# Scalings by roots a slot later, gate product and first taps on VectorE, short copies on ScalarE, and taps queued behind a slot's jobs

## The chip, the cores and the metric

The kernel runs on one core of a Trainium2 chip. The metric is device time in microseconds. Engines: TensorE (PE for its matmuls, PEld for its weight loads), VectorE (DVE), ScalarE (ACT), GpSimd (POOL) and SyncE (SP), which issues the DMAs here. Each engine runs its instructions in the order in which the program queued them and waits on semaphores for the results of other engines.

## The reference, cut to what matters

One layer of a streaming encoder for 256 prompt frames and 64 frames of a running stream, 2048 channels wide, in float32:

```python
h = rmsnorm(x, g_pre_mix)
p = h @ w_in
# group A: Conformer convolution on 1024 channels
u = p_val * sigmoid(p_gate)
u = causal_dwconv(u, state, w_dw, width 31) + b_dw
a = silu(layernorm per token and per group of 128 channels(u) * gn_g + gn_b)
# group B: gated DeltaNet, 8 heads of 128
qkv = silu(causal_dwconv(p_qkv, state, w_sc, width 4))
q, k = l2norm(q), l2norm(k)
o, s = gated delta rule in chunks (q, k, v, decay, beta, state)
b = rmsnorm per head(o) * onorm_g * silu(z)
x = x + rmsnorm(concat(a, b) @ w_out, g_post_mix)
h = rmsnorm(x, g_pre_ffn)
gate, up = split(causal_dwconv(h @ w_up, state, width 3) + b_ffn_dw)
x = x + rmsnorm((silu(gate) * up) @ w_down, g_post_ffn)
```

The outputs are x and the new states: the last 30 rows of u, the last 3 rows of q/k/v before their convolution, the delta rule's state, and the last 2 up-projected rows.

## The kernel before

Channels lie on the 128 partitions and the T = 320 frames (256 + 64) along the free axis. Each weight block of 128 x 1024 is loaded by DMA and split on the chip into a high part (`whi`, a ScalarE copy, L196) and a low part (`wlo`, a VectorE subtraction, L197); three matmuls a tile (L212, L213, L216) make a product near float32. These are the dense matmuls. A block of `w_in` has 48 of them, one of `w_out` in the mixer's stage 33.

**Jobs between the dense matmuls.** The mixer's small matmuls and transposes are not a stage of their own. They are generators ("jobs": `conv_tail`, `gdn_tail`, `pair` with `levels` and `post`) that advance between dense matmuls. `tick` counts the dense matmuls. At every 20th (`GAP`), a slot, it advances each job that is due, at most one step each, its TensorE instructions queued behind the last dense matmul and its priority raised. A `yield wait, g, t` says in how many dense matmuls the next step is due, and how many PSUM banks of the pools `ps_g` (4) and `ps_t` (2) that step takes; a step that finds too few waits for the next slot, and banks of `ps_t` count for the following slot too. The instructions of one engine are ordered at compile time by priority and estimated readiness; on the chip each engine then keeps to that order.

**Convolutions.** `conv_block(b)` computes gate and value of 128 channels. The normalisation's row factor `rb` multiplies both. The sigmoid is 0.5 tanh(x/2) + 0.5: VectorE scales the gate (L512), ScalarE takes tanh (L513), GpSimd makes the sigmoid and multiplies by `rb` (L514, L515), and VectorE multiplies by the value in PSUM (L521) into the buffer `ub`, whose 5 segments of 94 columns each begin with the 30 columns before it. GpSimd copies the saved rows (L520) and the overlaps (L523). The 31 taps (`cvt` and `odd`, two accumulators) and their sum are the list `taps`: the first on ScalarE (L536), the rest on VectorE (L538, L539, L533). `tick` hands out `pace` taps a slot: 3, 1 during the heads' projections, 4 at the end. `finish_conv(b - 3)` hands out what remains before the buffer is used again. `conv_tail(b)` waits until all taps are handed out, then 40 dense matmuls, transposes the sum (L554), takes mean and variance on VectorE, the root on GpSimd (L562, L563) and scales on ScalarE to `un` (L566); 100 dense matmuls later it transposes back (L570).

**Heads.** `qkv_block` evicts a q, k or v block to `qb`, copies its last rows to `nqkv` (L603, L604, GpSimd) and the saved rows into `qb` (L600, GpSimd) and applies 4 taps. `gdn_tail` transposes q, k, v, takes sums of squares on ScalarE, the inverse root and five products on GpSimd (L663 to L669), scales `kd`, `vh`, `kds` on ScalarE (L672 to L677), and 30 dense matmuls later multiplies keys by queries (`pk`, `pks`, L681, L685). When both heads of a pair are there, `pair` inverts a triangular matrix (`base_inverse`, `levels`: L755 to L800) and `post` runs the delta rule's two chunks (L827 to L884), takes a root on GpSimd (L893 to L897), scales `ot` on ScalarE (L899), and 120 dense matmuls later transposes the outputs (L909).

The blocks follow `PLAN`: z is a gate block, g the decays, h a head, c a convolution.

```python
PLAN = "z0 z1 g h0 h1 c0 h2 z2 h3 c1 z3 c2 h4 h5 c3 h6 h7 c4 z4 c5 z5 z6 c6 z7 c7"
```

After them come 15 blocks of `w_out` over the mixer outputs that are ready, then the rest of `w_out`, and the feed-forward part, which the change does not touch. From h4 on, a pair's first head forces the pair two before it on until it is `free`.

Of the kernel before, what the change touches and what calls it, by code (L numbers as in the profile page):

```python
# [9 lines left out]
F32 = mybir.dt.float32  # L10
F32R = mybir.dt.float32r
AF = mybir.ActivationFunctionType
ALU = mybir.AluOpType
# [4 lines left out]
P = 128  # L18
# [4 lines left out]
T = TP + TS  # L23
# [7 lines left out]
GAP = 20  # L31
# [8 lines left out]
LAG_NORM = 120  # L40
LAG_WAIT = 12
# [59 lines left out]
def trunk_kernel(ctx, tc, ins, outs):  # L101
    nc = tc.nc
    V, S, G, PE = nc.vector, nc.scalar, nc.gpsimd, nc.tensor
# [7 lines left out]
    dense = [None, 0]  # L111
# [3 lines left out]

    taps, pace = [], [3]

    def next_tap():
        left, fn = taps.pop(0)
        with tc.issue_after(dense[0]):  # L120
            fn()
        left[0] -= 1

# [18 lines left out]
    def tick(mm):  # L142
        dense[0] = mm.ins
        dense[1] += 1
        if dense[1] % GAP == 0:
            g, t0, behind = 0, held_t[0], dense[0]
            t = t0
            for job in sorted(jobs, key=lambda j: j[0]):
                if job[0] <= dense[1] and g + job[2] <= 4 and t + job[3] <= 2:
                    g += job[2]  # L150
                    t += job[3]
                    behind = advance(job, behind)
            held_t[0] = t - t0
            for _ in range(min(pace[0], len(taps))):
                next_tap()

    const = ctx.enter_context(tc.tile_pool(name="const", bufs=1))
    wst = ctx.enter_context(tc.tile_pool(name="wst", bufs=3))
# [12 lines left out]
    def pv(name, a=None, b=None):  # L171
        o, w = PAR[name]
        if a is None:
            return par[:, o:o + w]
        return par[:, o + a:o + (a + 1 if b is None else b)]
# [84 lines left out]
    rb = act.tile([P, T], F32, tag="rb", name="rb")  # L260
# [31 lines left out]
    with tc.tile_pool(name="xp", bufs=1) as xp:  # L292
# [25 lines left out]
        with tc.high_priority(offset=PRI_E):  # L318
# [25 lines left out]
            for k in range(KB):  # L344
                x = xt[k // 4][:, k % 4, :]
# [18 lines left out]
        for k0 in range(0, KB, 2):  # L364
            hi, lo = pre[k0 // 2]
            for ks in ((k0,), (k0 + 1,)) if k0 < 4 else ((k0, k0 + 1),):
                for wt in (hi, lo):
                    for k in ks:
                        for i, b in enumerate(FIRST):
                            ps = ready[b][:, 0:T]  # L370
                            o = (k - k0) * FW + i * P
                            w = wt[:, o:o + P]
# [15 lines left out]
    cb = pa.enter_context(tc.tile_pool(name="cb", bufs=2, reuse_waits="tile"))  # L388
# [103 lines left out]
    nqkv = const.tile([P, 24, 2, 3], F32, tag="nqkv", name="nqkv")  # L492

    ubufs = [cb.tile([P, 5, 94], F32, tag=f"ub{i}", bufs=1, name=f"ub{i}") for i in range(3)]
    for u in ubufs:
# [2 lines left out]
    def finish_conv(b):  # L500
        while any(left is lefts[b] for left, _ in taps):
            next_tap()
        finish(convs[b])
# [3 lines left out]
    def conv_block(b):  # L507
        psg_ = in_block(8 + b, "psgate")
        ub = ubufs[b % 3]
        with tc.high_priority(offset=PRI_E):  # L510
            sg = cb.tile([P, T], F32, tag="sg", bufs=1, name="sg")
            V.tensor_tensor(sg, psg_[:, 0:T], rb, ALU.mult)  # L512
            S.activation(sg, sg, AF.Tanh, scale=0.5)  # L513
            G.tensor_scalar(sg, sg, 0.5, 0.5, ALU.mult, ALU.add)  # L514
            G.tensor_tensor(sg, sg, rb, ALU.mult)  # L515
        psv = in_block(b, "psv")
        if b > 2:
            finish_conv(b - 3)
        with tc.high_priority(offset=PRI_E):
            G.tensor_copy(ub[:, 4, 0:30], pv("s_conv", b * 30, (b + 1) * 30))  # L520
            V.tensor_tensor(ub[:, :, 30:94], psv[:, 0:T].rearrange("p (s i) -> p s i", s=5),  # L521
                            sg.rearrange("p (s i) -> p s i", s=5), ALU.mult)
            G.tensor_copy(ub[:, 1:4, 0:30], ub[:, 0:3, 64:94])  # L523
        for i in range(2):
            nc.sync.dma_start(outs["conv"][:, b, i, :], ub[:, 3 + i, 64:94])

        cvt = cb.tile([P, 5, 64], F32, tag="cvt", bufs=3, name="cvt")
        odd = cb.tile([P, 5, 64], F32, tag="odd", bufs=1, name="odd")
        left = [32]

        def tap(t):
            if t == 31:
                return lambda: V.tensor_tensor(cvt, cvt, odd, ALU.add)  # L533
            x, acc, w = ub[:, :, t:t + 64], (cvt, odd)[t % 2], pv("w_dw", b * 31 + t)
            if t == 0:
                return lambda: S.activation(acc, x, AF.Identity, scale=w, bias=pv("b_dw", b))  # L536
            if t == 1:
                return lambda: V.tensor_scalar(acc, x, w, None, ALU.mult)  # L538
            return lambda: V.scalar_tensor_tensor(acc, x, w, acc, ALU.mult, ALU.add)  # L539

        lefts[b] = left
        taps.extend((left, tap(t)) for t in range(32))
        return cvt.rearrange("p s i -> p (s i)"), left

    def conv_tail(b, cvt, left):
        while left[0]:
            yield GAP, 0, 0
        yield LAG_CONV, 0, 1
        pt = ps_t.tile([P, 512], F32, tag="t", name="pt_c")
        st = cb.tile([P, 3, 6], F32, tag="bst", name="bst")  # L550
        gv = cb.tile([P, 3, 2], F32, tag="gvar", name="gvar")

        for c, o in enumerate((0, 128, 192)):
            PE.transpose(pt[:, c * P:(c + 1) * P], cvt[:, o:o + P], cv("ident"))  # L554
        for c in range(3):
            V.bn_stats(st[:, c, :], pt[:, c * P:(c + 1) * P])
            V.bn_aggr(gv[:, c, :], st[:, c, :])
        rs = cb.tile([P, 3], F32, tag="grs", name="grs")
        nm = cb.tile([P, 3], F32, tag="gnm", name="gnm")
        V.tensor_scalar(rs, gv[:, :, 1], EPS, None, ALU.add)  # L560
        V.tensor_scalar(nm, gv[:, :, 0], -1.0, None, ALU.mult)
        G.tensor_tensor(rs, rs, nhalf[:, 0:3], ALU.pow)  # L562
        G.tensor_tensor(nm, nm, rs, ALU.mult)  # L563
        un = cb.tile([P, 3, P], F32, tag="un", bufs=1, name="un")
        for c in range(3):
            S.activation(un[:, c, :], pt[:, c * P:(c + 1) * P], AF.Identity, scale=rs[:, c:c + 1], bias=nm[:, c:c + 1])  # L566
        yield LAG_STAT, 0, 1
        pt2 = ps_t.tile([P, 512], F32, tag="t", name="pt_c2")
        for c, o in ((2, 192), (1, 128), (0, 0)):
            PE.transpose(pt2[:, o:o + P], un[:, c, :], cv("ident"))  # L570
        af = cb.tile([P, T], F32, tag="t320", bufs=2, name="af")
        S.activation(af, pt2[:, 0:T], AF.Silu, scale=pv("gn_g", b), bias=pv("gn_b", b))
        split_mix(b, af)
# [22 lines left out]
    def qkv_block(b, dst, dsts, i):  # L596
        psq = in_block(16 + b, "psq")
        qb = qbufs[i % 2]
        with tc.high_priority(offset=PRI_E):
            G.tensor_copy(qb[:, 259:262], pv("s_qkv", b * 3, b * 3 + 3))  # L600
            V.tensor_tensor(qb[:, 3:259], psq[:, 0:TP], rb[:, 0:TP], ALU.mult)
            V.tensor_tensor(qb[:, 262:326], psq[:, TP:T], rb[:, TP:T], ALU.mult)
            G.tensor_copy(nqkv[:, b, 0, :], qb[:, 256:259])  # L603
            G.tensor_copy(nqkv[:, b, 1, :], qb[:, 323:326])  # L604
            cq = cb.tile([P, 323], F32, tag="cq", name="cq")
            S.activation(cq, qb[:, 0:323], AF.Identity, scale=pv("w_sc", b * 4))
            for t in range(1, 4):
                V.scalar_tensor_tensor(cq, qb[:, t:t + 323], pv("w_sc", b * 4 + t), cq, ALU.mult, ALU.add)
            S.activation(dst, cq[:, 0:TP], AF.Silu)
            S.activation(dsts, cq[:, TP + 3:TP + 3 + TS], AF.Silu)  # L610

# [14 lines left out]
    def gdn_tail(h, st, kq, vT):  # L626
        s = h % NS
# [39 lines left out]
        G.tensor_tensor(snb, rk, gate["nbeta"][:, 0:nch, h], ALU.mult)  # L667
        G.tensor_tensor(snb, snb, rk, ALU.mult)
        G.tensor_tensor(cc, rk, gate["beta"][:, 0:nch, h], ALU.mult)  # L669
        for c in range(nch):  # L670
            if c < 2:
                S.activation(kd[:, i0 + c, :], tk[c], AF.Identity, scale=skd[:, c:c + 1])  # L672
            else:
                for e in range(2):
                    r = slice(e * TS, (e + 1) * TS)
                    S.activation(kds[r, e, :], tk[c][r, :], AF.Identity, scale=skd[r, c:c + 1])
            S.activation(vh[:, i0 + c, :], tvs[c], AF.Identity, scale=irk[:, c:c + 1])  # L677
# [124 lines left out]
    def post(i, st):  # L802
# [39 lines left out]
        p = bank("ks", 4)  # L842
# [8 lines left out]
        p = outputs(0, vn0)  # L851
# [3 lines left out]
        p = bank("pvns", 1)  # L855
# [6 lines left out]
        p = bank("ks1", 4)  # L862
# [8 lines left out]
        p = bank("pos", 3)  # L871
# [11 lines left out]
        p = outputs(1, vn1)  # L883
# [11 lines left out]
        G.tensor_scalar(t1, t1, 1.0 / P, EPS, ALU.mult, ALU.add)  # L895
        G.tensor_tensor(t1, t1, nhalf[:, 0:NI], ALU.pow)
        G.tensor_tensor(t1, t1, rq, ALU.mult)  # L897
        for a in range(NI):
            S.activation(ot[:, a, :], ot[:, a, :], AF.Identity, scale=t1[:, a:a + 1])  # L899
        st["free"] = True  # L900
        yield LAG_NORM, 0, 2
        while any(zT[h] is None for h in hh_):
            yield GAP, 0, 2
        for s in range(2):
# [31 lines left out]
    for step in plan:  # L936
        kind, i = step[0], int(step[1:] or 0)
# [6 lines left out]
        elif kind == "h":  # L944
            if i % NS == 0:
# [4 lines left out]
                st = {}  # L950
# [32 lines left out]
    acc = None  # L983
# [144 lines left out]
    for q in range(NQ):  # L1128
# [5 lines left out]
        for j in range(QB):  # L1134
            b = q * QB + j
# [152 lines left out]
```

## Time and profile before

| | |
|---|---|
| median of 3 runs | 1509.2 us (1506.81 to 1511.67) |
| the profiled execution | 1509.19 us, span 1507.4 us |
| granted TensorE clock, mean | 0.995 |
| busy share of the span | PE 99%, PEld 97%, DVE 66%, ACT 48%, POOL 20% |
| HBM | 215.33 MB read, 7.12 MB written, 148 GB/s |

The profile lists, for each engine, what was busy when, how long it sat idle before an instruction and which other engine's instruction ended that idle time. A row of instructions in order of time gives its start and length in us, the engine, the line, the operation, the tiles (out<-in), the shapes and the count, and in brackets the idle time before it. A row of a group gives count, then busy us and mean ns of one, then the idle us before them. A row of waits gives who waited for whom: us in total, times, longest. The mixer's stage, in which all the changed lines run, lies between about 60 and 510 us.

### The profile page before, as it was taken

To read this page: it belongs to the slowest core of one execution; us is meant where nothing else is said; L and a number is where in the kernel's file an instruction comes from. 1 tells how busy PE (TensorE), PEld (TensorE's weight loads), DVE (VectorE), ACT (ScalarE), POOL (GpSimd) and SP (SyncE) were. 2 spreads that over 40 slices of the span, in tenths; PEclk is the share of its full clock that TensorE was granted. 3 is DMA by queue.
4 is the path that set the end of the run, shared out by engine and by line. 5 is a ranking of instruction groups with operands and counts; after the bars stand their busy time and mean duration, and the time that the engine had idled before them with its cause. 6 is when DMAs were issued, how large, how long until landed. Compare 5 with 4: busy or idle time off the path is not lost.

```text
span 1507.4 us, 27312 instructions
## 1 busy us (share of the span) xinstructions
PE 1486.2 (99%) x10609; PEld 1463.3 (97%) x10610; DVE 997.8 (66%) x1856; ACT 716.2 (48%) x1217; POOL 306.3 (20%) x492
## 2 busy tenths in 40 slices
PE   9999999999999999999999999999999999999998
PEld 8999998989899989999999999999999999999997
DVE  6798797879996568865435666545665545666554
ACT  7664555554454565544434444334444333444453
POOL 0333332441110000322002222001322101322101
PEclk9999999999999999999999999999999999999999
DMA  8335353455335654444454444455444455444453
GB/s 291 137 128 176 117 158 102 118 161 144 119 89 160 194 166 151 143 150 133 143 163 157 151 152 141 138 147 173 147 154 150 125 151 176 142 153 154 128 153 117
DMA packets 98281, 224.22 MB, mean 149 GB/s; under 512 B 18792, under 2 KB 39528, under 8 KB 98152
## 3 DMA queue, kind: packets, MB, share of 16 engines
q1 hardware_dynamic: 98008, 222.45, 46.4%
q8 instruction: 83, 1.36, 0.4%
q14 instruction: 46, 0.38, 0.1%
q10 hardware_dynamic: 144, 0.03, 0.0%
HBM read 215.33 MB, written 7.12 MB: 148 GB/s over the span
## 4 chain that ended last, share of the span: by engine, by line
PE 80%; DVE 11%; ACT 3%; issue 2%; DMA 2%; POOL 2%; SPq 0%; ACTq 0%; DVEq 0%
PE psu L216 13%; PE psu L213 13%; PE psu L212 13%; PE psdn L212 6%; PE psdn L213 6%; PE psdn L216 6%; DVE wlo L197 3%; PE psm L213 2%; PE psm L216 2%; PE psm L212 2%; PE psq L216 2%; PE psq L212 2%; PE psq L213 2%; PE psu L1081 1%; DVE odd L539 1%
## 5 line engine op out<-in xcount | busy, mean ns | idle before, releaser
L196 ACT CAST whi<-w 128x1024 fp32r<-128x1024 f32 (+2 forms) x440 | 412.9, 940 | 500.7 <-PE psu L213 168.5
L197 DVE TENSOR_TENSOR wlo<-w,whi 128x1024 fp32r<-128x1024 f32 (+2 forms) x440 | 478.0, 1087 | 200.8 <-ACT whi L196 125.8
L213 PE MATMUL psu<-lo,whi 128*128 128x320 f32 x1344 | 397.0, 309 | 0.0
L212 PE MATMUL psu<-hi,whi 128*128 128x320 f32 x1344 | 397.0, 309 | 0.0
L213 PEld LDWEIGHTS psu<-lo,whi 128*128 128x128 f32 x1344 | 252.3, 188 | 0.0
L212 PEld LDWEIGHTS psu<-hi,whi 128*128 128x128 f32 x1344 | 252.3, 188 | 0.0
L216 PE MATMUL psu<-hi,wlo 128*128 128x320 f32 x1344 | 224.4, 309 | 0.0
L1114 POOL COPY nffn<-fbuf 128x2 f32<-128x2 f32 x88 | 100.4, 1141 | 586.9 <-DVE fbuf L1112 583.7
L216 PEld LDWEIGHTS psu<-hi,wlo 128*128 128x128 f32 x1344 | 204.0, 188 | 0.0
L213 PE MATMUL psdn<-gl,whi 128*128 128x320 f32 x660 | 195.9, 310 | 0.0
L1112 DVE TENSOR_TENSOR fbuf<-psu,rb 128x256 f32<-128x256 f32 x88 | 37.4, 425 | 169.3 <-PE psu L216 169.3
L212 PE MATMUL psdn<-gh,whi 128*128 128x320 f32 x480 | 142.8, 309 | 0.0
L213 PEld LDWEIGHTS psdn<-gl,whi 128*128 128x128 f32 x660 | 123.9, 188 | 0.3
L212 PE MATMUL psq<-hh,whi 128*128 128x320 f32 x352 | 106.3, 315 | 0.0
L213 PE MATMUL psq<-hl,whi 128*128 128x320 f32 x352 | 104.1, 309 | 0.0
L212 PEld LDWEIGHTS psdn<-gh,whi 128*128 128x128 f32 x480 | 90.1, 188 | 0.0
L216 PE MATMUL psdn<-gh,wlo 128*128 128x320 f32 x480 | 89.9, 309 | 0.0
L216 PEld LDWEIGHTS psdn<-gh,wlo 128*128 128x128 f32 x480 | 75.3, 188 | 0.0
L212 PEld LDWEIGHTS psq<-hh,whi 128*128 128x128 f32 x352 | 66.1, 188 | 0.3
L213 PEld LDWEIGHTS psq<-hl,whi 128*128 128x128 f32 x352 | 66.1, 188 | 0.2
L539 DVE SCALAR_TENSOR_TENSOR cvt<-ub,par,cvt 128x320 f32<-128x320 f32 x120 | 66.1, 551 | 0.1
L539 DVE SCALAR_TENSOR_TENSOR odd<-ub,par,odd 128x320 f32<-128x320 f32 x112 | 62.1, 555 | 0.0
(360 smaller groups left out, 2516.7 us busy)
## 6 DMA issues: line engine op xcount, KB each, us to landing
w<-in_w_up SPq DMA_DIRECT2D x176, 512.0 KB, 3.7
w<-in_w_in SPq DMA_DIRECT2D x88, 512.0 KB, 3.7
w<-in_w_down SPq DMA_DIRECT2D x64, 384.0 KB, 3.1
w<-in_w_down SPq DMA_DIRECT2D x64, 320.0 KB, 2.9
w<-in_w_out SPq DMA_DIRECT2D x32, 320.0 KB, 2.9
w<-in_w_out SPq DMA_DIRECT2D x16, 384.0 KB
w<-in_w_first SPq DMA_DIRECT2D x6, 512.0 KB, 5.6
wtp<-wsp SPq DMA_DIRECT2D x4, 640.0 KB
```

Source lines behind the costliest of these rows:

```text
L196: S.copy(hi[:, 0:width], w[:, 0:width])
L197: V.tensor_tensor(lo[:, 0:width], w[:, 0:width], hi[:, 0:width].bitcast(F32), ALU.subtract)
L212: tick(PE.matmul(ps, wh, xh, start=(first and k0 + j == 0), stop=False))
L213: tick(PE.matmul(ps, wh, xl, start=False, stop=False))
L216: tick(PE.matmul(ps, lo[:, j * P:(j + 1) * P], xh, start=False, stop=(final and k0 + j == nk - 1)))
L539: return lambda: V.scalar_tensor_tensor(acc, x, w, acc, ALU.mult, ALU.add)
L1081: PE.matmul(pss[i][:, 0:T], wt[:, o:o + P], x, start=(k == 0 and n == 0), stop=(k == KB - 1 and n == 2))
L1112: V.tensor_tensor(buf[:, 2:258], psu[:, 0:TP], rb2[:, 0:TP], ALU.mult)
L1114: G.tensor_copy(nffn[:, b, 0, :], buf[:, 256:258])
```

## The change

- `next_tap` takes an instruction `front`, and queues the tap behind it. `tick` looks up the last VectorE instruction that the slot's jobs issued; the slot's taps go behind that one. Before, the edge named the last dense matmul.
- The product with the gate: (tanh + 1) x (value x 0.5 `rb`), two VectorE operations, with `rbh` = 0.5 `rb` made once on ScalarE. The two GpSimd operations go.
- The first tap goes from ScalarE to VectorE.
- The copies into `ub` and `qb`, and those to `nqkv` (two merged into one, after the taps), go from GpSimd to ScalarE.
- `conv_tail`, `gdn_tail` and `post` yield once more, for 12 dense matmuls (one slot), between the root on GpSimd and the scalings on ScalarE; in `post`, `free` is set before that and the lag after it is a slot shorter.

```diff
@@ -115,9 +115,11 @@
 
     taps, pace = [], [3]
 
-    def next_tap():
+    def next_tap(front=None):
         left, fn = taps.pop(0)
-        with tc.issue_after(dense[0]):
+        with ExitStack() as e:
+            if front is not None:
+                e.enter_context(tc.issue_after(front))
             fn()
         left[0] -= 1
 
@@ -145,14 +147,16 @@
         if dense[1] % GAP == 0:
             g, t0, behind = 0, held_t[0], dense[0]
             t = t0
+            n0 = len(nc.cur_bb.bb.instructions)
             for job in sorted(jobs, key=lambda j: j[0]):
                 if job[0] <= dense[1] and g + job[2] <= 4 and t + job[3] <= 2:
                     g += job[2]
                     t += job[3]
                     behind = advance(job, behind)
             held_t[0] = t - t0
+            front = next((i for i in reversed(nc.cur_bb.bb.instructions[n0:]) if i.engine == mybir.EngineType.DVE), None)
             for _ in range(min(pace[0], len(taps))):
-                next_tap()
+                next_tap(front)
 
     const = ctx.enter_context(tc.tile_pool(name="const", bufs=1))
     wst = ctx.enter_context(tc.tile_pool(name="wst", bufs=3))
@@ -492,6 +496,8 @@
     nqkv = const.tile([P, 24, 2, 3], F32, tag="nqkv", name="nqkv")
 
 
+    rbh = cb.tile([P, T], F32, tag="rbh", bufs=1, name="rbh")
+    S.activation(rbh, rb, AF.Identity, scale=0.5)
 
     ubufs = [cb.tile([P, 5, 94], F32, tag=f"ub{i}", bufs=1, name=f"ub{i}") for i in range(3)]
     for u in ubufs:
@@ -511,16 +517,16 @@
             sg = cb.tile([P, T], F32, tag="sg", bufs=1, name="sg")
             V.tensor_tensor(sg, psg_[:, 0:T], rb, ALU.mult)
             S.activation(sg, sg, AF.Tanh, scale=0.5)
-            G.tensor_scalar(sg, sg, 0.5, 0.5, ALU.mult, ALU.add)
-            G.tensor_tensor(sg, sg, rb, ALU.mult)
         psv = in_block(b, "psv")
         if b > 2:
             finish_conv(b - 3)
         with tc.high_priority(offset=PRI_E):
-            G.tensor_copy(ub[:, 4, 0:30], pv("s_conv", b * 30, (b + 1) * 30))
-            V.tensor_tensor(ub[:, :, 30:94], psv[:, 0:T].rearrange("p (s i) -> p s i", s=5),
-                            sg.rearrange("p (s i) -> p s i", s=5), ALU.mult)
-            G.tensor_copy(ub[:, 1:4, 0:30], ub[:, 0:3, 64:94])
+            hv = cb.tile([P, T], F32, tag="hv", bufs=1, name="hv")
+            V.tensor_tensor(hv, psv[:, 0:T], rbh, ALU.mult)
+            V.scalar_tensor_tensor(ub[:, :, 30:94], sg.rearrange("p (s i) -> p s i", s=5), 1.0,
+                                   hv.rearrange("p (s i) -> p s i", s=5), ALU.add, ALU.mult)
+            S.copy(ub[:, 4, 0:30], pv("s_conv", b * 30, (b + 1) * 30))
+            S.copy(ub[:, 1:4, 0:30], ub[:, 0:3, 64:94])
         for i in range(2):
             nc.sync.dma_start(outs["conv"][:, b, i, :], ub[:, 3 + i, 64:94])
 
@@ -533,7 +539,7 @@
                 return lambda: V.tensor_tensor(cvt, cvt, odd, ALU.add)
             x, acc, w = ub[:, :, t:t + 64], (cvt, odd)[t % 2], pv("w_dw", b * 31 + t)
             if t == 0:
-                return lambda: S.activation(acc, x, AF.Identity, scale=w, bias=pv("b_dw", b))
+                return lambda: V.tensor_scalar(acc, x, w, pv("b_dw", b), ALU.mult, ALU.add)
             if t == 1:
                 return lambda: V.tensor_scalar(acc, x, w, None, ALU.mult)
             return lambda: V.scalar_tensor_tensor(acc, x, w, acc, ALU.mult, ALU.add)
@@ -561,6 +567,7 @@
         V.tensor_scalar(nm, gv[:, :, 0], -1.0, None, ALU.mult)
         G.tensor_tensor(rs, rs, nhalf[:, 0:3], ALU.pow)
         G.tensor_tensor(nm, nm, rs, ALU.mult)
+        yield LAG_WAIT, 0, 1
         un = cb.tile([P, 3, P], F32, tag="un", bufs=1, name="un")
         for c in range(3):
             S.activation(un[:, c, :], pt[:, c * P:(c + 1) * P], AF.Identity, scale=rs[:, c:c + 1], bias=nm[:, c:c + 1])
@@ -597,15 +604,14 @@
         psq = in_block(16 + b, "psq")
         qb = qbufs[i % 2]
         with tc.high_priority(offset=PRI_E):
-            G.tensor_copy(qb[:, 259:262], pv("s_qkv", b * 3, b * 3 + 3))
+            S.copy(qb[:, 259:262], pv("s_qkv", b * 3, b * 3 + 3))
             V.tensor_tensor(qb[:, 3:259], psq[:, 0:TP], rb[:, 0:TP], ALU.mult)
             V.tensor_tensor(qb[:, 262:326], psq[:, TP:T], rb[:, TP:T], ALU.mult)
-            G.tensor_copy(nqkv[:, b, 0, :], qb[:, 256:259])
-            G.tensor_copy(nqkv[:, b, 1, :], qb[:, 323:326])
             cq = cb.tile([P, 323], F32, tag="cq", name="cq")
             S.activation(cq, qb[:, 0:323], AF.Identity, scale=pv("w_sc", b * 4))
             for t in range(1, 4):
                 V.scalar_tensor_tensor(cq, qb[:, t:t + 323], pv("w_sc", b * 4 + t), cq, ALU.mult, ALU.add)
+            S.copy(nqkv[:, b], qb[:, 192:326].rearrange("p (c i) -> p c i", c=2)[:, :, 64:67])
             S.activation(dst, cq[:, 0:TP], AF.Silu)
             S.activation(dsts, cq[:, TP + 3:TP + 3 + TS], AF.Silu)
 
@@ -667,6 +673,7 @@
         G.tensor_tensor(snb, rk, gate["nbeta"][:, 0:nch, h], ALU.mult)
         G.tensor_tensor(snb, snb, rk, ALU.mult)
         G.tensor_tensor(cc, rk, gate["beta"][:, 0:nch, h], ALU.mult)
+        yield LAG_WAIT, 1 + s, 1
         for c in range(nch):
             if c < 2:
                 S.activation(kd[:, i0 + c, :], tk[c], AF.Identity, scale=skd[:, c:c + 1])
@@ -895,10 +902,11 @@
         G.tensor_scalar(t1, t1, 1.0 / P, EPS, ALU.mult, ALU.add)
         G.tensor_tensor(t1, t1, nhalf[:, 0:NI], ALU.pow)
         G.tensor_tensor(t1, t1, rq, ALU.mult)
+        st["free"] = True
+        yield LAG_WAIT, 0, 0
         for a in range(NI):
             S.activation(ot[:, a, :], ot[:, a, :], AF.Identity, scale=t1[:, a:a + 1])
-        st["free"] = True
-        yield LAG_NORM, 0, 2
+        yield LAG_NORM - GAP, 0, 2
         while any(zT[h] is None for h in hh_):
             yield GAP, 0, 2
         for s in range(2):
```

## The prediction

> **What bounds the kernel now.** I read the page's first part, then the busy time of the mixer stage (60 to 500 us, where all of the changed code runs), then TensorE's rows around its idle gaps, then ScalarE's queue just before each gap.
>
> ```profile
> span 1507.4 us, 27312 instructions
> PE 1486.2 (99%) x10609; PEld 1463.3 (97%) x10610; DVE 997.8 (66%) x1856; ACT 716.2 (48%) x1217; POOL 306.3 (20%) x492
> ```
> ```profile
> 250.81:254.22 3.41, 3.41 (x14) 3.35 (x14) 1.80 (x4) 1.22 (x4) 0.00 (x0) 0.50 0.42 145
> 336.14:342.97 6.83, 6.68 (x46) 5.77 (x47) 5.24 (x15) 4.08 (x9) 0.26 (x1) 0.50 0.44 106
> 407.82:411.24 3.42, 3.42 (x36) 3.36 (x37) 3.36 (x7) 1.05 (x3) 0.00 (x0) 0.50 0.50 153
> 60.00:500.00 440.00, 427.60 (x3463) 416.70 (x3462) 367.13 (x807) 225.20 (x523) 119.19 (x183) 0.98 0.43 133
> ```
> Each of the last four lines is a stretch: its length, the busy time and (instructions) of PE, PEld, DVE, ACT and POOL, TensorE's granted clock, and what the DMAs did. TensorE sets the time; only its idle gaps and its slow stretches can be won. In the mixer stage it is idle 440.0 - 427.6 = 12.4 us, and in three stretches (13.66 us together) its granted clock is 0.50. The five gaps that matter here:
>
> ```profile
> 111.27 0.70 PE L685 MATMUL pks<-kqs 128*128 128x256 f32 x2 [1.81 <-ACT vh L677]
> 249.44 0.71 PE L827 MATMUL pvn<-vh,wtp 128*128 128x128 f32 x4 [2.45 <-ACT wtp L800]
> 251.43 0.47 PE L212 MATMUL psgate<-hh,whi 128*128 128x320 f32 x1
> 251.70 0.47 PE L213 MATMUL psgate<-hl,whi 128*128 128x320 f32 x1
> 254.46 0.31 PE L212 MATMUL psgate<-hh,whi 128*128 128x320 f32 x1
> 254.60 0.31 PE L213 MATMUL psgate<-hl,whi 128*128 128x320 f32 x1
> 336.12 1.22 PE L685 MATMUL pks<-kqs 128*128 128x256 f32 x2 [2.43 <-ACT vh L677]
> 407.32 0.24 PE L785 MATMUL px<-wtp,zq 32*32 32x32 f32 x2 [2.70 <-ACT zq L780]
> 420.65 0.68 PE L799 MATMUL px<-wtp,zq 64*64 64x64 f32 x8 [0.66 <-ACT zq L795]
> ```
> The bracket is the idle time and who ended it: ScalarE each time. I call them A to E; they sum to 10.05 us of the 12.4. Behind the three longest (B, C, D) the clock is halved: matmul starts there are 0.27 us apart (251.43, 251.70) against 0.14 to 0.15 (254.46, 254.60), so a halved stretch loses 45% (I take 0.147 us for a full-rate start): 13.66 x 0.45 = 6.1 us, 1.5 + 3.1 + 1.5. The gap A of 1.81 us is followed by none. So these gaps cost 16.2 us in all, 1.1% of the span.
>
> Why ScalarE was late, its rows around B, D, C and E:
>
> ```profile
> 247.99 1.16 ACT L566 ACTIVATE un<-pt_c,gnm,grs 128x128 f32<-128x128 f32 x3 [1.55 <-POOL gnm L563]
> 249.03 0.36 ACT L800 COPY wtp<-px 64x256 f32<-64x256 f32 x1
> 406.30 0.65 ACT L536 ACTIVATE cvt<-ub,par 128x320 f32<-128x320 f32 x1 [3.26 <-POOL ub L523]
> 406.98 0.28 ACT L780 COPY zq<-pz 32x160 f32<-32x160 f32 x1
> 334.93 0.37 ACT L672 ACTIVATE kd<-tkq,sc 128x128 f32<-128x128 f32 x1 [1.50 <-POOL sc L666]
> 419.05 1.16 ACT L566 ACTIVATE un<-pt_c,gnm,grs 128x128 f32<-128x128 f32 x3 [2.25 <-POOL gnm L563]
> 420.23 0.37 ACT L795 COPY zq<-pz 64x256 f32<-64x256 f32 x1
> ```
> ScalarE runs its queue in order. In B and E the copy that TensorE needs stands behind three scalings `un` that wait for GpSimd's root; in D behind the first tap, which waits for GpSimd's copy in `ub`; in A and C the awaited instructions are the scalings themselves. GpSimd is late because copies of three columns stand ahead of the root's last step, and because VectorE is late with `ub`:
>
> ```profile
> 246.20 0.82 POOL L603 COPY nqkv<-qb 128x3 f32<-128x3 f32 x1
> 247.45 0.50 POOL L563 TENSOR_TENSOR gnm<-gnm,grs 128x3 f32<-128x3 f32 x1
> 405.82 0.45 POOL L523 COPY ub<-ub 128x90 f32<-128x90 f32 x1 [6.28 <-DVE ub L521]
> ```
>
> **The change, part by part.** A slot is 20 dense matmuls, 20 x 0.147 = 2.9 us, and what its jobs put between them.
>
> *Convolution tail: `un` a slot later.* The same instructions, queued 2.9 us later on ScalarE. In B the copy L800 then need not stand behind a 1.55 us wait and 1.16 us of scalings: it moves from 249.03 to where that wait begins (247.99 - 1.55 = 246.44) and ends at 246.8. TensorE's gap begins at 249.44 - 2.45 = 246.99; of it I leave 0.3 us. E goes (-0.66). The second transposes (100 dense matmuls later) cover the shift itself; `un` keeps its PSUM bank a slot longer.
>
> *Heads: `kd`, `vh`, `kds` a slot later, and with them `pk` and `pks`,* since their lag counts from there. In C the scalings let go at 336.1 and `pks` is queued for 336.12 - 2.43 = 333.7; a slot later is 336.6. A is 1.81 us, under a slot. A goes; of C I leave 0.5 us, because its scalings are queued later too. On the other side each head holds its PSUM banks a slot longer and its pair starts 20 to 40 dense matmuls later. At h4 the code forces what is left of pair 0, so about three more steps are placed without a slot between them. The nearest rows are waits of such steps:
>
> ```profile
> PE pvns L856 <- DVE rhs L848: 0.6, 1, 0.6
> PE po L835 <- ACT vn L829: 0.5, 1, 0.5
> ```
> 3 x 0.55 = +1.6 us (between 0, if dense matmuls still lie between, and 3 x 1.8 = 5.4 us, were each as long as A; I take the rows of the same steps).
>
> *Norm of the outputs: scaling of `ot` a slot later,* and `free` set before it. The lag after it is shorter by 20, so the transposes keep their slot: 0.
>
> *Gate product and first tap.* GpSimd loses two operations a block. On VectorE the product with the value's PSUM stays one operation of the same shape; a two-operand product of the form of a tap (0.551 us) and the first tap (as L538, 0.540) come on top:
>
> ```profile
> L538 DVE TENSOR_SCALAR odd<-ub,par 128x320 f32<-128x320 f32 x8 | 4.3, 540 | 0.4 <-POOL ub L523 0.3
> L539 DVE SCALAR_TENSOR_TENSOR cvt<-ub,par,cvt 128x320 f32<-128x320 f32 x120 | 66.1, 551 | 0.1
> ```
> VectorE: 8 x (0.551 + 0.540) = +8.7 us on 367 busy of 440. That lies in its 73 us of idle time: 0 on the path, while it stays there (see the first rival). ScalarE sheds 8 x 0.65 = 5.2 us (the row at 406.30) and, in D, the tap ahead of L780. The new copy into `ub` waits for VectorE in its place, but VectorE's product no longer waits for GpSimd's two operations and can stand earlier in its queue, so I leave 0.3 us of D (at the other end it stays whole, 2.7 + 1.5). The one operation for `rbh` is some 0.5 us once, beside matmuls.
>
> *Short copies on ScalarE.* 8 x 2 into `ub` and 24 x 2 (the two `nqkv` copies merged) at between 0.21 us (row below) and 0.28 (L780 above):
>
> ```profile
> L771 ACT COPY wtp<-px 16x80 f32<-16x80 f32 x8 | 1.7, 212 | 3.2 <-DVE wtp L771 3.1
> POOL ub L520 <- DVE odd L539: 16.6, 4, 7.0
> POOL qb L600 <- DVE cq L608: 23.9, 8, 6.3
> ```
> 64 copies, about +14 us, on an engine busy 225 of 440 us: 0 by themselves. Their waits are the price. On GpSimd nobody stood behind them; on ScalarE the weight splits, the evictions and TensorE's next copy do. The copies into `qb` and `nqkv` wait for VectorE results that ScalarE's own `cq` and Silu await next to them, so I give them 0. The copy of the old rows into `ub` waits for the last tap of three blocks earlier, 16.6 us in 4 waits. Its share that reaches TensorE I take from ScalarE's waits for GpSimd now:
>
> ```profile
> ACT un L566 <- POOL gnm L563: 14.8, 7, 5.2
> ACT ot L899 <- POOL t L897: 11.6, 4, 4.0
> ACT vh L677 <- POOL sc L665: 10.6, 4, 3.2
> ACT kd L672 <- POOL sc L666: 8.1, 4, 3.0
> ACT cvt L536 <- POOL ub L523: 7.6, 5, 3.3
> ```
> 52.7 us of waits, behind which lie the 10.05 us of gaps: 19%. 16.6 x 0.19 = +3.2 us (bounds 0 and, were all of it to reach TensorE, 16.6).
>
> *Taps behind the slot's jobs.* The old edge named a matmul, and the taps aren't TensorE's, so it held nothing back; the new one keeps a slot's taps behind the last VectorE instruction of its jobs. A job's short operations no longer have 0.55 us taps between them (a gain that I count only as the certainty that A to E go), and VectorE can no longer run ahead with taps: 0, with the first rival as its bound.
>
> **Sum.** Gaps 10.05 - 1.1 left = -8.95; halved clock -6.1; forced steps +1.6; ScalarE's new waits +3.2: -10.2 us. The profiled execution took 1509.19 us with a span of 1507.4, so 1.8 lie around it, and it stands at the median of 1509.2. Span 1497.2, time **1499.0**.
>
> [...]
>
> **Rivals.** First, slower: VectorE becomes the bound. It has 73 - 9 = 64 us of slack. The stage's 44 blocks of 48 and 15 of 33 dense matmuls make 130 slots: 0.49 us a slot. If in the mean slot it sits idle longer than that, its taps held behind a job that awaits TensorE, the convolutions and then their transposes fall behind. Beyond 0.49 each tenth costs 13 us, so the 10.2 won are gone at 0.57; at 0.65 it is 130 x 0.16 = 20.8 over, and the time 1520. For it: taps now run far ahead,
>
> ```profile
> L533 DVE TENSOR_TENSOR cvt<-cvt,odd x8: 482/484/497, 124.8 to 462.2; 128x320 f32<-128x320 f32 x8
> L554 PE MATMUL pt_c<-cst,cvt x24: 270/272/329, 164.1 to 499.8; 128*128 128x128 f32 x24
> ```
> the last sum at 462.2 for transposes at 499.8, and that lead of 37 us goes. Against it: weight splits still fill the queue, and many slots have no job on VectorE. Chance 0.12.
>
> Second, no change: the waits move with the copies. If ScalarE takes over both 16.6 and 23.9 us and the same 19% arrives (7.7 instead of 3.2) and two new gaps reach 2.4 us with their half clock (2 x (2.4 + 1.5) = 7.8), the sum is -8.95 - 6.1 + 1.6 + 7.7 + 7.8 = +2.0: 1511, and with one such gap 1507. Chance 0.20.
>
> Third: the half clock stays although the gaps go: 1499.0 + 6.1 = 1505. The order of the rows (each stretch begins within 4 us of its gap's start) speaks against it. Chance 0.05.
>
> Fourth, better: no new wait at all: -15.05 and 1494, and with the small rest of the 12.4 us gone, 1492. Chance 0.10.
>
> **How the numbers follow.** The forecast, 1494 to 1504, has 0.53. Range 1490 to 1512: it takes in the second, third and fourth rival and leaves out most of the first. 0.3% is 4.5 us, about what a measurement here can tell from no change: faster means under 1504.7. Faster: forecast 0.53, the fourth 0.10, a little of the third, 0.65. Same: the rest of the third and most of the second, 0.21. Slower: the first and a rest of the second, 0.14.
>
> **What the next profile would show.** Right: no TensorE wait on `vh` L677's or `zq`'s successors above 1 us, fewer than two halved stretches, ScalarE's waits for GpSimd under 15 us, VectorE's busy time in the stage up by about 9 us. Wrong: gaps at the convolution transposes ended by VectorE (first rival), or long ScalarE waits at the copies into `ub` with TensorE behind them (second).

## The result, and the profile after

The changed kernel takes 1499.56 us (1498.79 to 1501.81), the kernel before on the same chip 1509.01: ratio 0.9938, interval 0.9925 to 0.9951. The forecast was 1499.0, in 1490 to 1512. The profiled execution took 1498.79 us with a span of 1496.9.

The first lines of the page, then the windows of the mixer's stage and of the one stretch with the clock at 0.50 (columns as in the prediction). The changed kernel's line numbers are 4 to 11 higher in this part.

```profile
span 1496.9 us, 27239 instructions
PE 1481.5 (99%) x10609; PEld 1460.3 (98%) x10610; DVE 1005.9 (67%) x1872; ACT 718.5 (48%) x1274; POOL 227.7 (15%) x388
...
334.58:337.99 3.41, 3.41 (x24) 3.35 (x17) 3.35 (x7) 0.95 (x3) 0.00 (x0) 0.50 0.07 10
60.00:500.00 440.00, 432.71 (x3534) 423.10 (x3533) 379.28 (x835) 229.42 (x575) 49.22 (x97) 1.00 0.44 136
```

TensorE's idle time in the stage fell from 12.4 to 440.0 - 432.7 = 7.3 us, the half clock from 13.66 to 3.41 us, which at 45% (matmul starts 0.27 us apart against 0.147) is 6.1 to 1.5. Together 18.5 to 8.8 us: -9.7 of the -10.5 us of span. TensorE's gaps above 0.4 us in that window:

```profile
176.11 0.40 PE L792 MATMUL px<-wtp,zq 32*32 32x32 f32 x13 [0.98 <-DVE zq L787]
195.80 0.46 PE L863 MATMUL pvns<-rhs,wtp 128*128 128x128 f32 x2 [0.69 <-DVE rhs L855]
196.98 1.16 PE L872 MATMUL ks<-sn,kq 128*128 128x128 f32 x8 [0.43 <-ACT sn L860]
199.10 0.68 PE L880 MATMUL pos<-rhs,kds 128*128 128x128 f32 x4 [0.82 <-ACT rhs L865]
333.80 0.77 PE L792 MATMUL px<-wtp,zq 32*32 32x32 f32 x15 [2.52 <-ACT zq L787]
406.01 0.40 PE L792 MATMUL px<-wtp,zq 32*32 32x32 f32 x13 [1.32 <-DVE zq L787]
```

(`px` is a small product in `levels`; its input `zq` is copied by ScalarE and by VectorE, half each. There is one such step of L792 for each of the four pairs of heads.) None of A, B, C and E is left; at the step where D stood, 1.32 us, ended by VectorE instead of ScalarE. A new gap of 2.52 us, with half clock, stands before the same step of the pair before that one. But what should have gone with them did not. ScalarE's waits for GpSimd in the same window, 45.1 us for these four before (14.8 + 11.6 + 10.6 + 8.1):

```profile
ACT un L573 <- POOL gnm L569: 18.6, 7, 4.0
ACT vh L684 <- POOL sc L671: 11.1, 3, 5.1
ACT kd L679 <- POOL sc L672: 9.9, 4, 3.4
ACT ot L908 <- POOL t L904: 8.3, 4, 3.2
```

47.9 us. The 2.52 us gap is of this kind, as its chain shows in order of time (VectorE's and GpSimd's rows, then ScalarE's):

```profile
329.98 1.22 DVE L201 TENSOR_TENSOR wlo<-w,whi 128x1024 fp32r<-128x1024 f32 x1
330.03 1.22 POOL L672 TENSOR_TENSOR sc<-sc,kdec 128x3 f32<-128x3 f32 x1
331.28 0.37 ACT L679 ACTIVATE kd<-tkq,sc 128x128 f32<-128x128 f32 x1 [3.44 <-POOL sc L672]
...
333.07 0.37 ACT L684 ACTIVATE vh<-tv,sc 128x128 f32<-128x128 f32 x1
333.46 0.28 ACT L787 COPY zq<-pz 32x160 f32<-32x160 f32 x1
```

The scalings `kd`, `kds` and `vh` (the rows left out are more of them) still stand in ScalarE's queue ahead of the copy `zq` that TensorE needs, and still wait for GpSimd. So the size was right and at least part of the reason was not.

### The profile page after: what moved, and what is told of

Its sections match the earlier page's. It is cut to its first block, busy times and chain, and to the rows that moved or that the text cites. A ratio compares the mean times of both kernels' runs of the same rounds, so it can differ in the third digit from the quotient of the medians.

```text
span 1496.9 us, 27239 instructions
## 1 busy us (share of the span) xinstructions
PE 1481.5 (99%) x10609; PEld 1460.3 (98%) x10610; DVE 1005.9 (67%) x1872; ACT 718.5 (48%) x1274; POOL 227.7 (15%) x388
## 4 chain that ended last, share of the span: by engine, by line
PE 89%; DVE 6%; DMA 2%; ACT 2%; issue 1%; POOL 1%; ACTq 0%; DVEq 0%; POOLq 0%
PE psu L220 13%; PE psu L217 13%; PE psu L216 13%; PE psdn L216 7%; PE psdn L217 6%; PE psdn L220 6%; PE psq L216 3%; PE psq L220 3%; PE psq L217 3%; DVE wlo L201 2%; PE psm L216 2%; PE psm L217 2%; PE psm L220 2%; PE psu L1089 1%; PE ps_first L378 1%
```

## The experiments

First theory: ScalarE's waits for GpSimd's roots hold up what TensorE needs, and the yields take the scalings out of the way. Rivals: the moves off GpSimd carry the gain; the order of the taps does; TensorE's steps only come later relative to their inputs; any reshuffle moves a few gaps.

All ratios are against the kernel before, on the same chip. "Lost" is TensorE's idle time in 60 to 500 us plus 45% of the half clock, of the profiled execution; "measured" is the ratio times 1509.

| kernel | ratio [95%] | measured us | idle + half clock = lost | lost, against before |
|---|---|---|---|---|
| before | 1 | 0 | 12.4 + 6.1 = 18.5 | 0 |
| changed | 0.9938 [0.9925, 0.9951] | -9.4 | 7.3 + 1.5 = 8.8 | -9.7 |
| yields alone | 0.9950 [0.9937, 0.9962] | -7.5 | 8.5 + 3.1 = 11.5 | -7.0 |
| all but the yields | 0.9957 [0.9943, 0.9971] | -6.5 | 10.4 + 1.5 = 11.9 | -6.6 |
| taps' order alone | 0.9980 [0.9971, 0.9989] | -3.0 | 11.9 + 3.1 = 15.0 | -3.5 |
| all but the taps' order | 0.9958 [0.9946, 0.9971] | -6.3 | 9.5 + 4.6 = 14.1 | -4.4 |
| yields and taps' order, no moves | 0.9977 [0.9965, 0.9988] | -3.5 | 9.7 + 3.1 = 12.8 | -5.7 |
| `un`'s yield alone | 1.0003 [0.9994, 1.0012] | +0.5 | 14.3 + 4.6 = 18.9 | +0.4 |
| products later alone | 0.9966 [0.9954, 0.9978] | -5.1 | 11.7 + 4.6 = 16.3 | -2.2 |
| neutral shift | 1.0005 [0.9996, 1.0014] | +0.8 | 14.5 + 3.1 = 17.5 | -1.0 |
| changed, two slots | 0.9957 [0.9945, 0.9970] | -6.5 | 10.8 + 0 = 10.8 | -7.7 |
| changed, `px` later | 0.9943 [0.9931, 0.9955] | -8.6 | 8.5 + 1.5 = 10.0 | -8.5 |
| changed, reciprocals on VectorE | 0.9867 [0.9852, 0.9881] | -20.1 | 0.1 + 0 = 0.1 | -18.4 |
| changed, Newton roots on VectorE | 0.9889 [0.9871, 0.9908] | -16.8 | 3.4 + 0 = 3.4 | -15.1 |

In all rows but two the lost time agrees with the measured one within 2 us. In these two the profiled execution was not typical: the profiled one with the products later took 1506.19 us against a median of 1503.52, and the runs without the moves spread from 1501.5 to 1508.5, the profiled one being the fastest of them.

**Parts and their complements.** *Yields alone* (the three hunks with `yield`, on the kernel before):

> The kernel before with the three new yields alone (un, kd/vh/kds and ot scaled a slot after their roots). By the prediction's sum this part carries the gaps A, B, C and E (-7.35 + 0.8 left), the half clock behind B and C (-4.6) and the forced steps (+1.6): about -9.5 us against before, and ScalarE's waits for GpSimd at un, ot, vh and kd fall from 45 us to under 20. Rival (the moves off GpSimd carry the gain, since in the changed kernel those waits stand at 48 us): within 3 us of before, waits unchanged. Second rival (any change of order shifts a few gaps): anything between -5 and +5 us, with gaps of 2 us or more at other places than A to E.

-7.5 us. The gaps at `pks` are gone and 0.5 us is left at the step of B, near the 0.3 us forecast; at D's step, which this kernel should leave as it is, the gap has grown to 3.56 us and is ended by VectorE's half of `zq`. But ScalarE waits for `un` 17.0, `vh` 14.3, `ot` 11.3 and `kd` 6.8 us: 49.4, not under 20. The time followed the theory, the queue did not.

*All but the yields* (the changed kernel without these hunks):

> The changed kernel without the three yields: moves and the order of the taps alone. By the prediction's sum: gap D and its half clock go (-3.9) and ScalarE's new waits come (+3.2): about -1 us against before. Rival (moves carry it): -7 us or more. Second rival: between -5 and +5 us.

-6.5 us, far more than the -1 that I had given the rest. The waits of TensorE show why the parts do not add up:

```profile
PE pks L691 <- ACT vh L683: 0.6, 1, 0.6
PE pvn L833 <- ACT wtp L806: 0.3, 1, 0.3
```

Without any yield A is down to 0.65 us, B to 0.25, and C and D are below 0.3: either part alone takes most of A, B and C, so the second one finds little left of them. This kernel has other gaps instead, up to 1.75 us, and ScalarE's four waits for GpSimd stand at 53.4 us.

*Taps' order alone* (`next_tap(front)` on the kernel before) and *all but it*:

> The kernel before with only a slot's taps queued behind its jobs' last VectorE instruction. By the prediction 0 by itself (within 2 us of before). Rival (VectorE's order makes the jobs' results early): -5 us or more, the last VectorE step before each GpSimd root (gnm) some 1 us earlier after the transposes. Its slow side: later taps, +5 us or more, with TensorE waiting at the convolution transposes.

> The changed kernel without that order of the taps. By the prediction -10 us against before, like the changed kernel. Rival (the order carries it): -5 us or less gain. If taps between a job's short operations are what delays the roots, gnm comes about 1 us later after the transposes than in the changed kernel.

-3.0 and -6.3: the order is worth some 3 us both ways, neither 0 as I had it nor the main part. In the kernel without it a gap of 2.65 us with half clock stands at D's step, ended by VectorE's half of `zq`. The order can make a job's end earlier. The second convolution's last VectorE step before the root, behind its transposes, in the kernel before and with the order alone (the transposes of the kernel before start at 239.78):

```profile
245.69 0.16 DVE L561 TENSOR_SCALAR gnm<-gvar 128x3 f32<-128x3 f32 x1
```
```profile
240.58 0.55 PE L558 MATMUL pt_c<-cst,cvt 128*128 128x128 f32 x3
243.83 0.16 DVE L565 TENSOR_SCALAR gnm<-gvar 128x3 f32<-128x3 f32 x1
```

5.9 us before, 3.3 with the order, and gap B behind that root shrinks to 0.25 us. Over the eight convolutions the mean from transposes to `gnm` moves only from 4.5 to 4.2 us, though, and in the changed kernel it is 4.6 with the order and 4.8 without, not 1 us apart: it helps at some places and costs at others. Whether an earlier `gnm` accounts for the 3 us stays open.

*Yields and taps' order, no moves:*

> The kernel before with the three yields and the order of the taps, but gate product, first tap and short copies where they were. If the parts add (yields -7.2, taps' order -3.0): about -10 us, like the changed kernel with its moves, which then are worth nothing. If the moves are what frees gap D: -6 us at most, with a gap of 2 us or more at px behind the first tap on ScalarE.

-3.5 us. Not the sum (-10.5), and less than the yields alone. Three gaps of 2.24, 2.53 and 3.15 us stand at `px` of two levels. The first tap is in front of one of them alone, for 0.65 us and without a wait of its own: the 2.24 us gap stands behind `vh`, which waits 7.10 us for GpSimd, further scalings, two weight copies and that tap. The 2.53 us one stands behind `kd` and `vh` that wait 3.75 us for GpSimd, and the 3.15 us one waits for VectorE's half of `zq`. So the moves are needed for the full gain, for another reason than gap D alone. Why yields and order together do worse than the yields alone I can only place (these three gaps, in an execution of 1501.51 us where the median is 1506.35), not explain.

**What a yield does.** Three kernels take it apart. `un`'s yield alone; `LAG_PAIR = 50` for 30 without any yield, so that `pk` and `pks` come a slot later and the scalings stay; and in the changed kernel two slots (`yield LAG_WAIT + GAP`) for convolutions and heads.

> The kernel before with the convolution's yield alone (un a slot after its root). First theory: gaps B and E (2.45 and 0.66 us) and the half clock behind B go: -4.6 us. Rival (later products are what counts): within 2 us of before. Since un still waits 17.0 us for GpSimd with all three yields, the rival has the better odds.

> The kernel before with LAG_PAIR 50 for 30 alone: pk and pks a slot later, the scalings where they were. Rival of the yields (the later products are what counts): gaps A and C (1.81 and 2.43 us) gone, half clock behind C gone, -4 to -7 us against before, near the -7.2 us of the kernel with the yields alone. First theory (the scalings out of ScalarE's way): no more than A and C's gaps for a start and new gaps elsewhere, within 3 us of before.

> The changed kernel with the scalings of convolutions and heads two slots after their roots (LAG_WAIT + GAP). In the changed kernel ScalarE still waits 48 us for GpSimd: the roots are done 4.2 to 8.7 us after the convolution's transposes, a slot is only 2.9 us and more. First theory (ScalarE's waits for roots make TensorE's gaps): those waits fall below 20 us, the gaps before 505 us from 7.1 to 4 us or less, time -2 to -4 us against the changed kernel (about 1496). Rival (it matters only that pk, pks and the next steps are due later than their inputs, not that ScalarE waits): waits fall as well, but the time stays within 2 us of the changed kernel, or is up to 4 us longer through pairs that start later.

`un`'s yield alone gains nothing (1.0003; C is gone, and other gaps up to 2.10 us came), and gap B is there to the hundredth:

```profile
248.74 1.16 ACT L567 ACTIVATE un<-pt_c,gnm,grs 128x128 f32<-128x128 f32 x3 [1.55 <-POOL gnm L563]
249.78 0.36 ACT L801 COPY wtp<-px 64x256 f32<-64x256 f32 x1
250.19 0.71 PE L828 MATMUL pvn<-vh,wtp 128*128 128x128 f32 x4 [2.45 <-ACT wtp L801]
```

The same wait of 1.55 us, the same three scalings ahead of the copy, as in the kernel before at 247.99. With two slots, second convolution, transposes and scalings:

```profile
237.44 0.55 PE L560 MATMUL pt_c<-cst,cvt 128*128 128x128 f32 x3
...
242.15 1.16 ACT L573 ACTIVATE un<-pt_c,gnm,grs 128x128 f32<-128x128 f32 x3 [1.90 <-POOL gnm L569]
```

ScalarE is idle, waiting for `gnm`, from 240.25 on, 2.8 us after the transposes; two slots are at least 5.9 us. The scalings are not held to the slot. In the code the edge that a slot gives goes to TensorE's instructions alone. My reading is that a scaling is placed in ScalarE's queue where the compiler expects its root to be ready, and that GpSimd is later on the chip (the roots end 4.2 to 8.7 us after the transposes in the changed kernel); the compiler's estimate is not on record. What a yield moves is the next TensorE step. That alone, `pk` and `pks` a slot later, gives -5.1 of the -7.5 us: A is down to 0.54 us, and B and C are gone. The rest of the yields' gain is not settled: `ot`'s yield alone was not tried. Two slots instead of one lose some 3 us of the gain (the intervals just overlap): no half clock, but gaps of 2.00 us (twice) and 1.74 us at steps of later pairs and convolutions.

**Is it reshuffling?**

> The kernel before with LAG_STAT 120 for 100: the convolution's second transposes a slot later, which nothing on the path waits for. A measure of what any shift of the order does: if parts act by their mechanism, within 1.5 us of before with gaps A to E in place; if any reshuffle moves gaps of 2 us and their half clock, some other set of gaps and up to 4 us either way.

1.0005: no gain or loss. A, B and D stand at full length (1.84, 2.45, 2.70), C shrank to 0.43 and two others grew to 2.09 and 1.98. Some shift of gaps is there, but it isn't what makes 5 to 10 us.

**Are ScalarE's waits the cause?** The two theories now left: a wait of ScalarE for GpSimd, or just a step due too early. `px` of the 32-wide level a slot later (one more `GAP` in that yield):

> The changed kernel with the step px of the 32-wide level due one slot later (LAG_WAIT + GAP in that yield alone). Three of its gaps stand there, waiting for zq: 0.98, 2.52 and 1.32 us, and its one stretch of half clock (1.5 us) behind the second. Rival theory (a gap is a TensorE step due too early): these gaps and the half clock go, -6 us against the changed kernel less about 1 for pairs that start later, so some 1494. First theory (ScalarE's queue makes the gaps): ScalarE's waits for GpSimd stay at 48 us, gaps move to other places, within 2 us of the changed kernel.

-8.6, within 1 us of the changed kernel. Its three gaps at that step and the half clock behind them are gone, and as many others came, one with half clock: 1.88 us at `pvns`, 1.86 at the first block of `w_out`, 1.32 at `px` of the next level, 1.25 at the convolution's transposes, ScalarE's waits for GpSimd 50.5. Moving a step does not shorten the chain that is late. Taking GpSimd out of it does:

```diff
-        G.tensor_tensor(rs, rs, nhalf[:, 0:3], ALU.pow)
-        G.tensor_tensor(nm, nm, rs, ALU.mult)
+        V.reciprocal(rs, rs)
+        V.scalar_tensor_tensor(nm, gv[:, :, 0], -1.0, rs, ALU.mult, ALU.mult)
```

and likewise for the heads (`irk`, `skd`) and the output norm. This kernel leaves out the square root, so its outputs are other numbers; it serves to measure time alone.

> The changed kernel with what ScalarE waits for taken off GpSimd: the roots of convolutions, heads and output norm are reciprocals on VectorE, and the products that the scalings need follow there (so the root itself is left out; some 100 short VectorE operations more, about +10 us of its busy time). First theory (ScalarE's waits for GpSimd make TensorE's gaps): these waits go from 48 us to near 0, the gaps before 505 us from 7.1 to 4 us or less, and the time falls by 3 us or more against the changed kernel. Rival (the gaps come where a TensorE step is due before its inputs, whoever makes them): waits go to near 0 and the time stays within 2 us of the changed kernel.

1488.62 us, 11 us below the changed kernel. The stage's window:

```profile
60.00:500.00 440.00, 439.89 (x3601) 431.00 (x3600) 390.08 (x896) 240.25 (x587) 8.95 (x37) 1.00 0.47 143
```

TensorE is idle 0.1 us of 440, there is no half clock, and no wait of ScalarE for GpSimd is left; the longest waits of its weight copies are now for TensorE (22.6 us for `psq`). That is the half of the first theory that stands: take the roots off GpSimd, and TensorE's gaps go. It is not that VectorE became faster without GpSimd beside it: a split of a whole block takes 1215 ns, for 1219 in the changed kernel, and a tap 542, for 548. The gaps that VectorE ended (0.98 and 1.32 us) went too. How the late roots led to those is not traced; VectorE's waits for ScalarE's weight copies fell from 25.5 to 10.3 us. The experiment takes away GpSimd's late roots and ScalarE's waits for them together; which of the two would do alone stays open.

**A version that keeps the root.** The same, with the root from a first guess (one operation on the number's bits as an integer) and three Newton steps:

```diff
+    def root(y, x, a):
+        V.tensor_scalar(y.bitcast(mybir.dt.int32), x.bitcast(mybir.dt.int32), -0.5, 1597463007.0, ALU.mult, ALU.add)
+        for _ in range(3):
+            V.tensor_tensor(a, y, y, ALU.mult)
+            V.scalar_tensor_tensor(a, a, -0.5, x, ALU.mult, ALU.mult)
+            V.scalar_tensor_tensor(y, a, 1.5, y, ALU.add, ALU.mult)
```

> As the kernel with reciprocals on VectorE, but with the root itself there: a first guess from the number's bits and three Newton steps, ten short VectorE operations for each root (20 roots, some 200 operations; at about 0.1 us from start to start +20 us of VectorE time on 380 of 440). First theory (ScalarE's waits for GpSimd make the gaps): waits stay near 0, and as long as VectorE keeps up the time is near the 1488.6 us of the kernel with reciprocals, at most 1493. Rival (VectorE becomes the bound): TensorE waits for VectorE at the transposes of the convolutions or at the products, and half of the gain or more goes: 1495 or above.

1493.33 us (1492.48 to 1493.76), ratio 0.9889 to before: with nothing left out, 6 us below the changed kernel and 16 below the one before. The time lies 0.3 us above the 1493 that I had set as the limit. VectorE is busy 407 of 440 us, and the rival shows itself in small:

```profile
60.00:500.00 440.00, 436.59 (x3571) 426.45 (x3570) 406.68 (x1072) 236.40 (x582) 7.80 (x37) 1.00 0.46 140
```
```profile
PE pt_c L567 <- DVE cvt L546: 1.5, 3, 0.8
PE pos L888 <- ACT rhs L873: 0.8, 1, 0.8
PE px L776 <- ACT zh L771: 0.5, 1, 0.5
PE ks L880 <- ACT sn L868: 0.4, 1, 0.4
```

TensorE waits for the convolutions' taps (1.5 us), which it never did in the kernel before. It did so in three of the kernels above: 1.75 us without the yields, 1.25 with `px` later, 0.8 with two slots.

## Why the prediction was right, point by point

- **The sum.** Forecast -10.2 us of span, measured -10.5. Its parts: gaps net of new ones -8.95 + 1.6 + 3.2 = -4.15, measured -5.1; half clock -6.1, measured -4.6, since one new gap of 2.52 us brought a stretch back. The two errors, 1.0 and 1.5 us, cancel in part; the other 0.8 us of the 10.5 lie outside these two sums.
- **Luck in the total.** By the prediction's prices the yields alone were worth -9.5 us and all the rest -1. Measured were -7.5 and -6.5, and -9.4 together, because either part takes most of A, B and C. The sum was right because it was added up over the gaps, and the gaps went; it was wrong about which part takes them. That it came within 1 us of the measured time is partly luck.
- **Which gaps.** A, B, C and E went and D shrank to 1.32 us, where 0.3 had been left of it. That new ones would come was in the sum only as prices; they came as 2.52 and 0.98 us at `px` of other pairs. Waits above 1 us there had been named as a sign against the prediction, and two came, 2.52 and 1.32 us.
- **"The same instructions, queued 2.9 us later on ScalarE": this step failed.** `un` alone shows no effect, and the waits that should have fallen under 15 us stand at 47.9. B went because its step came a slot later while `un` stayed in front (`px` starts 3.4 us after the convolution's transposes in the kernel before, 7.1 after in the changed one). In the changed kernel ScalarE's copy still ends only at 249.63, and `pvn` is due then:

```profile
247.66 0.81 ACT L573 ACTIVATE un<-pt_c,gnm,grs 128x128 f32<-128x128 f32 x2 [1.69 <-POOL gnm L569]
248.91 0.47 ACT L573 ACTIVATE un<-pt_c,gnm,grs 128x128 f32<-128x128 f32 x1
249.27 0.36 ACT L807 COPY wtp<-px 64x256 f32<-64x256 f32 x1
```
```profile
245.99 0.67 PE L806 MATMUL px<-wtp,zq 64*64 64x64 f32 x8
249.68 0.71 PE L834 MATMUL pvn<-vh,wtp 128*128 128x128 f32 x4
```

- **`pk` and `pks` later** was right as written, A and C went, and it is the larger part of what the yields give (-5.1 of -7.5).
- **Gate product and gap D.** Right in kind. The value block's last matmuls and the product into `ub`, before and after:

```profile
398.56 1.33 PE L216 MATMUL psv<-hh,wlo 128*128 128x320 f32 x8
405.26 0.49 DVE L521 TENSOR_TENSOR ub<-psv,sg 128x320 f32<-128x320 f32 x1
```
```profile
391.04 1.33 PE L220 MATMUL psv<-hh,wlo 128*128 128x320 f32 x8
396.08 0.52 DVE L526 SCALAR_TENSOR_TENSOR ub<-sg,hv 128x320 f32<-128x320 f32 x1
```

  From the start of the one to the end of the other it was 7.2 us and is 5.6, and `zq` is no longer behind a first tap. VectorE's busy time grew by 1005.9 - 997.8 = 8.1 us over the whole run (forecast 8.7; 12.2 in the stage's window, into which more of the work now falls), but the first tap with its bias takes 0.60 us, not 0.54.
- **Short copies.** Forecast 0.21 to 0.28 us each and 16.6 us of inherited waits with 3.2 on the path. Measured, group rows:

```profile
L614 ACT COPY nqkv<-qb 128x6 f32<-128x6 f32 x20 | 3.8, 188 | 0.0
L607 ACT COPY qb<-par 128x3 f32<-128x3 f32 x19 | 3.4, 182 | 0.0
L529 ACT COPY ub<-ub 128x90 f32<-128x90 f32 x8 | 2.1, 269 | 10.0 <-DVE ub L526 9.9
L528 ACT COPY ub<-par 128x30 f32<-128x30 f32 x5 | 1.1, 221 | 2.4 <-DVE odd L545 2.4
```

  The wait for the old taps shrank to 2.4 us, the one for the product is 9.9. None of TensorE's gaps above 0.4 us stands behind either. The 3.2 us were not paid there; what came instead is at `px`, 2.52 + 0.98 us.
- **Forced steps.** Forecast +1.6 us. The three gaps from 195.8 to 199.1 are 0.69 + 0.43 + 0.82 = 1.94 us, against 0.57 + 0.53 there before: +0.84.
- **The taps' order** I had at 0; it is worth 3 us alone and 3 on top of the rest. The lead that it takes was read rightly: the last sum of taps now starts at 487.1 for transposes at 489.4, 2.3 us ahead instead of 37. It cost nothing in the changed kernel, at 379 busy us of 440, and 1.5 us at 407; but other kernels with this order paid 0.8 to 1.75 us at 376 to 380, so the busy time alone does not tell.
- **The rivals.** VectorE as the bound did not happen. "The waits move with the copies" happened once (2.52 us with half clock), though not through the copies. The half clock did not stay without its gaps: the one stretch left begins 0.78 us behind the end of the gap of 2.52 us.

## What to carry to other kernels

Before you price a delay, ask which engine's queue it is tied to: here an extra yield moved the steps of TensorE, and the scalings on ScalarE kept their waits for GpSimd (47.9 us after 45.1). Shifting the consumers can win (5.1 us for `pk` and `pks` here) or only move the gaps (`px`). If an engine keeps to its queue and waits there for a late one (in the changed kernel ScalarE sat idle for 1.69 us until 247.66, the last 1.0 us with the input of its copy `wtp` done, and took the scalings first), try to take the late engine out of the chain and to let the engine that makes the input finish the job: here that gave 6 us on top of the shifts with the square root kept, and 11 without it. And run the one-part kernels: -7.5 and -6.5 us for a part and its complement do not add to the -9.4 of both, since both take the same gaps.

## What the runs showed of the hardware

**The half clock and the length of a gap.** In the profile of the kernel before, the clock stands at 0.50 in three stretches ahead of the last matmul: from 250.81, 336.14 and 407.82 us on, 3.41, 6.83 and 3.42 us long. Each begins behind a TensorE gap, of 2.45 us (246.99 to 249.44), 2.43 (333.69 to 336.12) and 2.70 (404.62 to 407.32), and 1.37, 0.02 and 0.50 us after the gap's end. In the changed kernel the one stretch, 3.41 us from 334.58 on, begins 0.78 us after the end of the gap of 2.52 us (331.28 to 333.80). The other gaps above 0.9 us between matmuls in these two profiles, 1.81 and 1.00 us before and 0.98 and 1.32 after, have no half clock behind them.

The length of the gap alone does not sort the other kernels: with `px` later there is one stretch of half clock and no wait of TensorE above 1.9 us, with two slots there are gaps of 2.00 us and no half clock. What else decides, and why the stretch at 336.14 is 6.83 us long and the others 3.41 or 3.42, stays open.

**GpSimd's operations of three columns.** Their length varies. In the changed kernel a product of 3 columns took 1.22 us (330.03), beside VectorE's weight split of 1.22 us (329.98); the two ended within 0.05 us of each other. The product of the same shape before it took 0.19 us (329.87). In the kernel before, the 24 copies at L603 took from 0.18 to 5.21 us, the longest from 286.15 us on, beside an unbroken row of VectorE instructions; the copy after it took 0.18 us (291.31), and VectorE was at work then too. On ScalarE the short copies into `qb` and `nqkv` took 0.18 and 0.19 us in the mean of the changed kernel. Whether such long operations are why GpSimd's roots come late, no run here separates.
